# A decoder layer on one core: the factors of four norms spread by float32r high and low diagonals of 512 columns, and the recurrence's statistics later

## The chip, the cores and the metric

The kernel runs on one core of a Trainium2 chip. The metric is device time in microseconds of one execution. A core has TensorE (PE: matmuls into PSUM, with weight loads, PEld, that overlap them), VectorE (DVE), ScalarE (ACT), GpSimd (POOL) and SyncE (SP, which here issues DMAs). Each engine works through its own queue in order and waits on semaphores for the others.

## What is computed

One layer for a sequence of 512 tokens with 1024 features: a half-step SwiGLU FFN of 2816 hidden features, a mixer, and a second half-step FFN. Each of the three is wrapped in two RMS norms, one on its input and one on its output before it is added to the stream. Inside the mixer the recurrence's output and the attention's output, 512 features each, have a norm of their own:

```python
def rms_norm(x, g):
    y = x * lax.rsqrt(jnp.mean(x * x, axis=-1, keepdims=True) + 1e-6)
    return y * g

def hybrid_mixer(h, ...):
    x_lru, gate_lru, q, k, v = split(h @ w_in)
    y_lru = rg_lru(x_lru, ...) * gelu(gate_lru)          # 512 features
    y_attn = sliding_window_sink_attention(q, k, v, sinks)
    y = concatenate([rms_norm(y_lru, g_lru_out), rms_norm(y_attn, g_attn_out)])
    return y @ w_o

x = x + 0.5 * rms_norm(swiglu(rms_norm(x, ffn1_pre_g), ...), ffn1_post_g)
x = x + rms_norm(hybrid_mixer(rms_norm(x, mix_pre_g), ...), mix_post_g)
x = x + 0.5 * rms_norm(swiglu(rms_norm(x, ffn2_pre_g), ...), ffn2_post_g)
```

All inputs and the output are fp32.

## The kernel before

**Layout and precision.** Activations are kept turned: features on the 128 partitions, 512 tokens along the free axis (`T`; `NB` = 4 blocks of 128 tokens, `KD` = 8 chunks of 128 features, `KC` = 4). To keep fp32 precision at float32r's matmul rate, each operand is split into a high part (rounded to float32r) and a low part (the rest), and a product is three matmuls: high by high, high by low, low by high (`mm3`).

**Norms.** A norm's factor belongs to a token, that is, to a column in this layout, so a number for each token has to reach all 128 partitions. `InvRms` does that for half the tokens (256) at a time:
- `stats` takes a bank of PSUM and turns the sums of squares (`acc`, features on partitions) into means with tokens on partitions: one matmul of one column (fp32, with `acc` as the weights) for each block of 128 tokens.
- `invert` takes the square root (ACT) and the reciprocal (DVE), and makes the diagonal: the identity times the factor, 128 x 256 in fp32 (DVE).
- `spread` multiplies the diagonal with a matrix of ones in one fp32 matmul of 256 columns, which leaves every token's factor on all partitions. In the profile an fp32 matmul appears as two records.

`Next` is the norm ahead of a sub-layer. Its inputs go through the products unscaled; the factors are copied to a tile `R` (ACT, `Next.spread`) and multiplied in afterwards (DVE). There are three: `n1` (name `a`, bank `rms_x`, whose statistics `InvRmsX.early` takes from sums over the rows of x), `mx` (the mixer's input) and `n2` (`f2`). The recurrence's norm, `lru`, uses `InvRms` as well, without a copy: DVE multiplies `hl` by the PSUM bank. The norms on the sub-layers' outputs (`Residual`) use `InvRms` too.

**Order.** All engines' orders are written out by hand: an engine executes its instructions in the order in which the program issues them. `Weights` (`W`) streams weights from HBM into a ring of raw tiles (SP's queue); a unit's `cast` (ACT) makes the high part and `tensor_sub` (mostly DVE) the low part. `W.fill(n)` prepares units until n are ready beyond those taken, `W.round` casts one, `W.take` hands one out; the next raw load is issued when the last unit of a raw tile has its low part.

**Around the recurrence's norm.** The output product `y @ w_o` runs over eight output chunks c. For the first five (`EARLY`) the attention's half is multiplied first (`wo_attn`: high parts by both weight parts for each k, then low parts). For c = 0 to 2 together these are 36 matmuls, then come the statistics of `lru` (both halves) and `W.fill(3)`; then c = 3 (12 matmuls), the two spreads and, on DVE and ACT, the scaled outputs `ylh` and `yll` of the recurrence; then c = 4 (12 matmuls), and then the recurrence's half for all five (`mm3` over k = 0, 1, and then 2, 3). The rest of `w_o` and the next sub-layer's start are in `boundary`.

Of the kernel before, what the change touches and what calls it, by code (L numbers as in the profile page):

```python
# [23 lines left out]
KC = C // P  # L24
# [98 lines left out]
def tile_layer(ctx: ExitStack, tc: tile.TileContext, out: bass.AP, **ins: bass.AP):  # L123
    nc = tc.nc
    pe, dve, act, pool, sync = nc.tensor, nc.vector, nc.scalar, nc.gpsimd, nc.sync

    const = ctx.enter_context(tc.tile_pool(name="const", bufs=1))
# [3 lines left out]
    small = ctx.enter_context(tc.tile_pool(name="small", bufs=4))  # L131
# [5 lines left out]
    ALL = slice(0, T)  # L137
# [348 lines left out]
    def preload(func):  # L486
        act.activation(dummy, eps, func)
# [9 lines left out]
    def col(name, i):  # L497
        return colrange(name)[:, i:i + 1]
# [40 lines left out]
    def square(src, sl, name, scale=1.0):  # L539
        sq = wt(f"sq_{name}")[:, sl]  # L540
        act.activation(sq, src, AF.Square, scale=scale)  # L541
        return sq

    class InvRms:


        def __init__(self, accs, mean, half, name, eps=eps):
            self.accs, self.mean, self.half, self.name, self.eps = accs, mean, half, name, eps

        def stats(self):  # L550
            self.ps = ps = bank(f"rms_{self.name}")
            for i in range(2):
                b = 2 * self.half + i
                for j, a in enumerate(self.accs):
                    pe.matmul(ps[:, i:i + 1], a[:, b * P:(b + 1) * P], self.mean, start=j == 0, stop=j == len(self.accs) - 1)
            self.invert(ps[:, :2])

        def invert(self, ms, scale=1.0):
            n = self.name
            rms = small.tile([P, 2], F32, tag="rms", name=f"rms_s{n}")  # L560
            act.activation(rms, ms, AF.Sqrt, bias=self.eps, scale=scale)
            rs = small.tile([P, 2], F32, tag="rs", name=f"rs_{n}")
            dve.reciprocal(rs, rms)
            self.dg = wt(f"dg_{n}", T)[:, :2 * P].rearrange("p (a b) -> p a b", a=2)
            dve.tensor_tensor(self.dg, ident.unsqueeze(1).to_broadcast([P, 2, P]), rs.unsqueeze(2).to_broadcast([P, 2, P]), op=ALU.mult)

        def spread(self):
            o = self.ps[:, T // 2:]
            pe.matmul(o, ones, self.dg.rearrange("p a b -> p (a b)"), start=True, stop=True)
            return o  # L570


    def stream():
# [10 lines left out]
    def x_high(x, src, gain, sl):  # L584
        act.activation(x[0][:, sl], src, AF.Copy, scale=gain)

    def x_low(x, src, gain, sl):
        dve.scalar_tensor_tensor(x[1][:, sl], src, gain, x[0].bitcast(F32)[:, sl], op0=ALU.mult, op1=ALU.subtract)
# [13 lines left out]
    class Next:  # L602


        def __init__(self, name, pre=None, gain=None):
            self.name, self.pre = name, pre
            self.gain = gain or (lambda c: col(pre, c))
            self.t = {}
            self.xs = x_parts(name)
            self.acc = tmp.tile([P, T], F32, tag="acc", name=f"acc_n{name}", bufs=3)  # L610
            self.rms = [InvRms([self.acc], mean_d, h, f"n{name}{h}") for h in range(2)]
            self.R = None

        def high(self, c, h):
# [10 lines left out]
                    dve.tensor_add(self.acc, self.acc, square(xT[c], ALL, f"n{self.name}{c}"))  # L625

        def stats(self):
            for h in range(2):
                self.rms[h].stats()

        def spread(self):
            if self.R is None:
                self.R = big.tile([P, T], F32, tag="R", name=f"R_{self.name}")
                for h in range(2):
                    act.copy(self.R[:, HALF[h]], self.rms[h].spread())

        def sums(self, k):

# [555 lines left out]
        hi, lo, raw = piece(j, i)  # L1194
        eng.tensor_sub(lo, raw, hi.bitcast(F32))

    class InvRmsX(InvRms):


        def early(self):  # L1200
            b = 4 * self.half
            ss = small.tile([P, 2], F32, tag="ss", name=f"ss_{self.name}")
            sx = ssx[:, b:b + 4].rearrange("p (b h) -> p b h", h=2)
# [6 lines left out]
    n1.rms = [InvRmsX(None, None, h, f"x{h}") for h in range(2)]  # L1210


    warm = bank("warm")
# [54 lines left out]
    for r in n1.rms:  # L1268
        r.early()
# [50 lines left out]


    gw, home = {}, []
    v4 = lambda t: t.rearrange("p (a b) -> p a b", a=NB)
    up8 = t2k("up8", U8).rearrange("p (a b) -> p a b", a=NB)
    up8f = up8.rearrange("p a b -> p (a b)")

# [311 lines left out]
    hl = us_  # L1638
# [218 lines left out]
    def add_square(ci):  # L1857
        if ci == 0:
            act.activation(accl, hl[0], AF.Square)
        else:  # L1860
            dve.tensor_add(accl, accl, square(hl[ci], ALL, f"l{ci}"))

    for ci in range(KC):
        add_square(ci)
    preload(AF.Sqrt)
    lrms = [InvRms([accl], mean_c, h, f"lru{h}") for h in range(2)]

    res = Residual("r2", lambda c: col("mix_post_g", c))
    EARLY = KD - LATE

    def wo_attn(cs):
        ks = range(KC, KD)
        for k in ks:
            for c in cs:
                for part in ws[c]:
                    pe.matmul(banks[c], part[:, k, :], ysp[k][0], start=k == KC and part is ws[c][0], stop=False)
        for c in cs:
            for k in ks:
                pe.matmul(banks[c], ws[c][0][:, k, :], ysp[k][1], start=False, stop=False)

    ws, banks = [], []
    for c in range(EARLY):
        ws.append(W.take(0))
        banks.append(bank(f"wo{c}"))
        if c < EARLY - 3:
            continue
        wo_attn(range(c + 1) if c == EARLY - 3 else [c])
        if c == EARLY - 3:
            for l in lrms:
                l.stats()  # L1890
            W.fill(3)
        if c == EARLY - 2:
            bcs = [l.spread() for l in lrms]
            for ci in range(KC):
                for h in range(2):
                    dve.tensor_mul(hl[ci][:, HALF[h]], hl[ci][:, HALF[h]], bcs[h])
                y = t2k(f"ylh{ci}", F32R), t2k(f"yll{ci}", F32R)
                x_high(y, hl[ci], col("g_lru_out", ci), ALL)
                x_low(y, hl[ci], col("g_lru_out", ci), ALL)
                ysp[ci] = y  # L1900
    for k in (0, 1):
        for c in range(EARLY):
            mm3(banks[c], ws[c], k, ysp[k], False, False)
# [202 lines left out]
```

## Time and profile before

| | us |
|---|---|
| median of 3 runs | 839.75 |
| lowest, highest | 839.74, 840.31 |
| the profiled execution | 839.52 |
| its span, first to last instruction | 837.6 |
| TensorE busy | 829.3 |
| VectorE busy | 730.5 |
| ScalarE busy | 520.0 |
| GpSimd busy | 166.4 |

The profiled execution's mean granted TensorE clock is 0.998 of full speed. In the rows of the timeline the first column is the start in us from the span's start, the second the time in us, then engine, line, operation, out<-in, sizes and how many instructions the row merges; square brackets hold the idle time of the engine just before it and what ended it. Records of matmuls overlap, because they are pipelined. Busy times are averages over stages with different limits; what counts at a place is which engine comes last there.

### The profile page before, as it was taken

The page shows a single profiled execution, that of the slowest core. Times are in us where ns is not written, and L with a number is a line of the kernel's source. Part 1 is how long each engine was busy: PE and PEld are TensorE (multiplying, and loading weights), DVE is VectorE, ACT ScalarE, POOL GpSimd, SP SyncE. Part 2 cuts the span into 40 slices and gives each one's busy share as a digit, 9 for nine tenths or more (in the row PEclk, how much of TensorE's full clock was granted, in tenths as well). Part 3 has the DMA queues.
Part 4 walks back from the last instruction along what each step waited for, and adds up shares of the span by engine and source line. Part 5 has one row for each costly group of instructions (what it writes and reads, how often), then busy time and mean ns, then how long its engine had stood idle before and what let it go on. Part 6 is the DMA issues. An engine that isn't in the chain of part 4 may idle for free.

```text
span 837.6 us, 11902 instructions
## 1 busy us (share of the span) xinstructions
PE 829.3 (99%) x4252; PEld 705.7 (84%) x4252; DVE 730.5 (87%) x1036; ACT 520.0 (62%) x813; POOL 166.4 (20%) x188
## 2 busy tenths in 40 slices
PE   9999999999999999999999999999999999999996
PEld 8988888888888898987788899888888888888885
DVE  4989799998989978888789589997999799898996
ACT  6656656676666654556797446545757667676562
POOL 2022000140320325414531042002005023032001
PEclk9999999999999999999999999999999999999999
DMA  7376408398595797522511130657339939769742
GB/s 253 102 266 236 147 10 302 97 264 261 124 259 183 186 280 235 181 93 78 163 47 51 51 124 30 129 173 251 110 114 244 312 85 256 238 155 259 299 142 101
DMA packets 121851, 144.22 MB, mean 172 GB/s; under 512 B 24184, under 2 KB 76736, under 8 KB 121280
## 3 DMA queue, kind: packets, MB, share of 16 engines
q1 hardware_dynamic: 107824, 112.91, 42.0%
q0 software_dynamic: 13824, 30.42, 16.5%
q8 instruction: 33, 0.54, 0.3%
q14 instruction: 26, 0.21, 0.1%
q10 hardware_dynamic: 144, 0.13, 0.0%
HBM read 100.45 MB, written 39.32 MB: 167 GB/s over the span
## 4 chain that ended last, share of the span: by engine, by line
PE 96%; DVE 2%; DMA 1%; SPq 0%; issue 0%; ACT 0%; DVEq 0%; ACTq 0%
PE ab L968 10%; PE aa L968 10%; PE db L968 5%; PE da L968 5%; PE yaa L1362 3%; PE bb L968 3%; PE ba L968 3%; PE ya L1362 3%; PE yda L1362 2%; PE aa L898 1%; PE a_first L1230 1%; PE yab L1945 1%; PE yab L1946 1%; PE yab L1947 1%; PE yea L1362 1%; PE yba L1362 1%
## 5 line engine op out<-in xcount | busy, mean ns | idle before, releaser
L1140 POOL DMA_DIRECT2D yr_a<-stage x36 | 31.6, 1013 | 176.8 <-ACT stage L1137 155.9
L1140 POOL DMA_DIRECT2D yp_b<-stage x42 | 36.5, 1046 | 147.0 <-ACT stage L1137 118.2
L1961 POOL DMA_DIRECT2D yp_b<-stage x8 | 4.3, 546 | 65.3 <-ACT stage L1960 64.8
L691 POOL TENSOR_TENSOR acca_r<-acca_r,sq_r 128x512 f32<-128x512 f32 x6 | 9.0, 1498 | 40.0 <-ACT sq_r L541 39.9
L529 PE MATMUL an<-xh_mx,whi_xl 128*128 128x256 f32 x64 | 15.9, 288 | 0.0
L530 PE MATMUL an<-xh_mx,wlo_xl 128*128 128x256 f32 x64 | 15.5, 283 | 0.0
L2061 ACT ACTIVATE ysq<-yp 128x512 f32<-128x512 f32 (+1 forms) x8 | 4.9, 606 | 16.7 <-DVE yp L2054 16.7
L2064 POOL TENSOR_TENSOR last<-yp,grow 128x512 f32<-128x512 f32 x3 | 3.9, 1293 | 56.2 <-DVE yp L2054 56.2
L511 PE MATMUL gt<-xh_mx,whi_gt 128*128 128x512 f32 x32 | 14.3, 447 | 0.0
L1399 POOL DMA_DIRECT2D yp_a<-zy x16 | 8.8, 555 | 25.4 <-DMA rows_a<-yr_a 17.2
L511 PE MATMUL pq<-xh_mx,whi_q 128*128 128x512 f32 x32 | 12.8, 400 | 0.0
L511 PE MATMUL pub<-xh_f,whi_bu 128*128 128x512 f32 x32 | 12.6, 395 | 0.0
L513 PE MATMUL gt<-xh_mx,wlo_gt 128*128 128x512 f32 x32 | 12.6, 394 | 0.0
L511 PE MATMUL pgb<-xh_f,whi_bg 128*128 128x512 f32 x32 | 12.6, 393 | 0.0
L512 PE MATMUL gt<-xl_mx,whi_gt 128*128 128x512 f32 x32 | 12.5, 392 | 0.0
L512 PE MATMUL pq<-xl_mx,whi_q 128*128 128x512 f32 x32 | 12.5, 391 | 0.0
L513 PE MATMUL pq<-xh_mx,wlo_q 128*128 128x512 f32 x32 | 12.5, 390 | 0.0
L513 PE MATMUL pgb<-xh_f,wlo_bg 128*128 128x512 f32 x32 | 12.5, 390 | 0.0
L513 PE MATMUL pub<-xh_f,wlo_bu 128*128 128x512 f32 x32 | 12.5, 390 | 0.0
L512 PE MATMUL pub<-xl_f,whi_bu 128*128 128x512 f32 x32 | 12.5, 390 | 0.0
L512 PE MATMUL pgb<-xl_f,whi_bg 128*128 128x512 f32 x32 | 12.5, 389 | 0.0
L1362 PE MATMUL ya<-whi_ad,hha 128*128 128x512 f32 x32 | 12.4, 389 | 0.0
(2018 smaller groups left out, 3412.7 us busy)
## 6 DMA issues: line engine op xcount, KB each, us to landing
yp_b<-stage POOLq DMA_DIRECT2D x50, 256.0 KB, 9.2
yr_a<-stage POOLq DMA_DIRECT2D x44, 256.0 KB, 9.8
h_a<-za SPq DMA_DIRECT2D x16, 256.0 KB
h_b<-zb SPq DMA_DIRECT2D x16, 256.0 KB
hxb<-h_b SPq DMA_DIRECT2D x16, 256.0 KB
hxa<-h_a SPq DMA_DIRECT2D x6, 512.0 KB
xn<-in_x SPq DMA_DIRECT2D x8, 256.0 KB
raw_ad<-in_ffn_w_down SPq DMA_DIRECT2D x2, 1024.0 KB
```

Of the source, the lines that this page charges most:

```text
L511: pe.matmul(ps, hi[:, k, :], xh, start=start, stop=False)
L512: pe.matmul(ps, hi[:, k, :], xl, start=False, stop=False)
L513: pe.matmul(ps, lo[:, k, :], xh, start=False, stop=stop)
L529: pe.matmul(ps[:, sl], hi[:, k, :], xh, start=k == 0 and not goes_on, stop=False, skip_group_check=True)
L530: pe.matmul(ps[:, sl], lo[:, k, :], xh, start=False, stop=False, skip_group_check=True)
L691: eng.tensor_add(acc, acc, square(part, ALL, f"{self.name}{c}"))
L898: pe.matmul(o, w[:, k, js], x, start=first and i + j + k == 0, stop=k == 3 and i == 2, skip_group_check=True)
L968: pe.matmul(b[tb], x[:, blk], w[:, k, :], start=first and q + k + j == 0, stop=q + k == 2 and j == 2, skip_group_check=True)
L1140: pool.dma_start(o, st, accum_op=ALU.add)
L1230: pe.matmul(banks[j][:, HALF[0]], ws[j][part][:, k, :], n1.xs[k][xpart][:, HALF[0]], start=k == 0 and part == xpart, stop=stop and k == KD ...
L1362: pe.matmul(o, x[:, blk], a[:, k, :], start=start and j == 0, stop=stop and j == 2, skip_group_check=True)
L1399: (pool if q % 2 else sync).dma_start(chunks[32 * q:32 * (q + 1), :, i * P:(i + 1) * P], turned[32 * i:32 * (i + 1), :, q])
```

## The change

For the three `Next` norms and for `lru` a new class, `InvRmsRows`, takes all 512 tokens at once. One bank instead of two, four statistics matmuls into it, one square root of four columns, one reciprocal. The factor is then split into a float32r high part (the diagonal made from the factor itself is rounded as it is written) and a low part (factor less rounded factor), and two diagonals of 128 x 512 in float32r are made. Spread is two float32r matmuls of 512 columns into the same bank, added up. `ones` becomes a float32r tile; the output norms keep `InvRms` with the same values read as fp32. `R` is filled by one ACT copy of 512 columns instead of two of 256, and `hl` is multiplied in one DVE operation of 512 columns instead of two.

```diff
-    ones = filled("ones", P, 1.0)
+    ones = const.tile([P, P], F32R, name="ones")
+    dve.memset(ones.bitcast(F32), 1.0)
...
+    class InvRmsRows:
+        def __init__(self, acc, mean, name):
+            self.acc, self.mean, self.name = acc, mean, name
+        def stats(self):
+            self.ps = ps = bank(f"rms_{self.name}")
+            for b in range(NB):
+                pe.matmul(ps[:, b:b + 1], self.acc[:, b * P:(b + 1) * P], self.mean, start=True, stop=True)
+            self.invert(ps[:, :NB])
+        def invert(self, ms, scale=1.0):
+            n = self.name
+            rms, rs, low = (small.tile([P, NB], F32, tag=t, name=f"{t}_{n}", bufs=1) for t in ("rms4", "rs4", "rl4"))
+            high = small.tile([P, NB], F32R, tag="rh4", name=f"rh4_{n}", bufs=1)
+            act.activation(rms, ms, AF.Sqrt, bias=eps, scale=scale)
+            dve.reciprocal(rs, rms)
+            dve.tensor_copy(high, rs)
+            dve.tensor_sub(low, rs, high.bitcast(F32))
+            self.dg = [wt(f"d{i}_{n}", T, F32R) for i in "hl"]
+            for d, r in zip(self.dg, (rs, low)):
+                dve.tensor_tensor(v4(d), ident.unsqueeze(1).to_broadcast([P, NB, P]), r.unsqueeze(2).to_broadcast([P, NB, P]), op=ALU.mult)
+        def spread(self):
+            for i, d in enumerate(self.dg):
+                pe.matmul(self.ps, ones, d, start=i == 0, stop=i == 1)
+            return self.ps
...
     class Next:
-            self.rms = [InvRms([self.acc], mean_d, h, f"n{name}{h}") for h in range(2)]
+            self.rms = InvRmsRows(self.acc, mean_d, f"n{name}")
...
-                for h in range(2):
-                    act.copy(self.R[:, HALF[h]], self.rms[h].spread())
+                act.copy(self.R, self.rms.spread())
```

`InvRmsX` derives from the new class and adds its row sums for all four blocks in one operation. Around the recurrence's norm the order changes as well: one `w_o` unit is cast (`W.round`) ahead of the square root's table load; the statistics come two matmuls into c = 3, the spread with the recurrence's outputs two matmuls into c = 4; of the two units that `W.fill(3)` prepared, one is finished behind c = 2 and the other behind the outputs.

```diff
     for ci in range(KC):
         add_square(ci)
+    W.round()
     preload(AF.Sqrt)
-    lrms = [InvRms([accl], mean_c, h, f"lru{h}") for h in range(2)]
+    lrms = InvRmsRows(accl, mean_c, "lru")
...
-    def wo_attn(cs):
+    def wo_attn(cs, between=lambda: None):
         for k in ks:
             for c in cs:
                 for part in ws[c]:
                     pe.matmul(banks[c], part[:, k, :], ysp[k][0], ...)
+            if k == KC:
+                between()
...
-        wo_attn(range(c + 1) if c == EARLY - 3 else [c])
         if c == EARLY - 3:
-            for l in lrms:
-                l.stats()
-            W.fill(3)
-        if c == EARLY - 2:
-            bcs = [l.spread() for l in lrms]
-            (the outputs, product in halves)
+            wo_attn(range(c + 1))
+            W.fill(2)
+        elif c == EARLY - 2:
+            wo_attn([c], lrms.stats)
+        else:
+            wo_attn([c], spread_lru)
+    W.fill(1)
```

`spread_lru` spreads and makes the outputs as before, with the product over all 512 columns.

More of the change, by code (lines that the diff above doesn't have):

```diff
@@ L568, in spread @@
             o = self.ps[:, T // 2:]
-            pe.matmul(o, ones, self.dg.rearrange("p a b -> p (a b)"), start=True, stop=True)
+            pe.matmul(o, ones.bitcast(F32), self.dg.rearrange("p a b -> p (a b)"), start=True, stop=True)
             return o
+    class InvRmsRows:
[21 more added lines that the diff above has]
+            return self.ps
     def stream():
@@ L1208, in stats @@
             self.ps = bank(f"rms_{self.name}")
[L1210 removed]
+    n1.rms = InvRmsX(None, None, "x")
     warm = bank("warm")
@@ L1879, in wo_attn, with spread_lru @@
                 pe.matmul(banks[c], ws[c][0][:, k, :], ysp[k][1], start=False, stop=False)
+    def spread_lru():
+        bc = lrms.spread()
+        for ci in range(KC):
+            dve.tensor_mul(hl[ci], hl[ci], bc)
+            y = t2k(f"ylh{ci}", F32R), t2k(f"yll{ci}", F32R)
+            x_high(y, hl[ci], col("g_lru_out", ci), ALL)
+            x_low(y, hl[ci], col("g_lru_out", ci), ALL)
+            ysp[ci] = y
     ws, banks = [], []
```

22 lines of the change are left out of this document (6 added, 16 removed).

## The prediction

> **What bounds the kernel now.** I read the page first (engines, chain), then the waits of TensorE, then the timeline of each engine around the four norms.
>
> ```profile
> span 837.6 us, 11902 instructions
> ...
> PE 829.3 (99%) x4252; PEld 705.7 (84%) x4252; DVE 730.5 (87%) x1036; ACT 520.0 (62%) x813; POOL 166.4 (20%) x188
> ...
> DMA packets 121851, 144.22 MB, mean 172 GB/s; under 512 B 24184, under 2 KB 76736, under 8 KB 121280
> ...
> PE 96%; DVE 2%; DMA 1%; SPq 0%; issue 0%; ACT 0%; DVEq 0%; ACTq 0%
> ```
>
> The chain that ended last is 96% TensorE, and TensorE is busy 99% of the span. So a shorter TensorE slot shortens the run, as long as no other engine becomes late in its place; what is done on VectorE (DVE), ScalarE (ACT) or GpSimd (POOL) counts only where TensorE then waits. In the view of TensorE's waits only one lies inside the run, at the norm that the change moves:
>
> ```profile
> PE rms_lru L555 <- DVE acc_lru L1861: 0.3, 1, 0.3
> ```
>
> The steady pace of a 128x512 float32r matmul, and the slots of the four fp32 spreads (each row: four records, two for each half), from the timeline of TensorE:
>
> ```profile
> 469.02 0.39 PE L511 MATMUL wo<-ylh,whi_wo 128*128 128x512 f32 x1
> ...
> 476.95 0.39 PE L513 MATMUL wo<-ylh,wlo_wo 128*128 128x512 f32 x1
> ...
> 28.61 1.02 PE L569 MATMUL rms_x<-dg_x,ones 128*128 128x256 f32 x4
> 29.59 0.28 PE L530 MATMUL a_first<-xh_a,wlo_first 128*128 128x256 f32 x1
> ...
> 373.05 1.02 PE L569 MATMUL rms_nmx<-dg_nmx,ones 128*128 128x256 f32 x4
> 374.15 0.40 PE L512 MATMUL pv<-xl_mx,whi_kv 128*128 128x512 f32 x1
> ...
> 465.39 1.02 PE L569 MATMUL rms_lru<-dg_lru,ones 128*128 128x256 f32 x4
> 466.49 0.40 PE L1876 MATMUL wo<-attn,wlo_wo 128*128 128x512 f32 x1
> ...
> 530.85 1.03 PE L569 MATMUL rms_nf<-dg_nf,ones 128*128 128x256 f32 x4
> 531.95 0.40 PE L512 MATMUL pub<-xl_f,whi_bu 128*128 128x512 f32 x1
> ```
>
> From 469.02 to 476.95 us are 35 steps of back-to-back matmuls: 0.2266 us each, though each record is 0.39 us long, since they overlap. So slots have to be read from start to start. The last row of each pair is the second matmul after the spread; between lie the spread and one ordinary matmul.
>
> **The change part by part.**
>
> *Spread.* Removed are two fp32 matmuls of 256 columns for each norm. Their slot is 374.15 - 373.05 - 0.23 = 0.87 us; the recurrence's (466.49 - 465.39) and the last norm's (531.95 - 530.85) come to the same. In the first norm the neighbours have 256 columns and a step of 0.12 (half of 0.23): 29.59 - 28.61 - 0.12 = 0.86. Added are two float32r matmuls of 512 columns, 2 x 0.2266 = 0.45. Saving: 3 x 0.42 + 0.41 = 1.67 us on TensorE. The weights are `ones` before and after.
>
> For this price the Trainium skill has a rule ("TensorE: Matmul & The Clock Gate", section Back-to-back issue gap): a sustained stream with N=512 runs at about 131 ns for each matmul. By it the two added matmuls would cost 0.26, and the sum would gain another 0.76; the trace shows 0.2266 for exactly this shape, and that is used.
>
> *Statistics.* Four one-column fp32 matmuls stay. Only in the recurrence's norm (`lru`) do they move: behind two more matmuls of c=3.
>
> ```profile
> 369.37 0.95 PE L555 MATMUL rms_nmx<-mean_d,acc_nmx 128*128 128x1 f32 x8
> ...
> 370.50 0.40 PE L512 MATMUL pk<-xl_mx,whi_kv 128*128 128x512 f32 x1
> ...
> 460.46 0.84 PE L1879 MATMUL wo<-yal,whi_wo 128*128 128x512 f32 x3
> 461.60 1.05 PE L555 MATMUL rms_lru<-mean_c,acc_lru 128*128 128x1 f32 x8 [0.30 <-DVE acc_lru L1861]
> ...
> 462.84 0.40 PE L1876 MATMUL wo<-attn,wlo_wo 128*128 128x512 f32 x1
> ```
>
> ```profile
> 459.27 2.27 DVE L1861 TENSOR_TENSOR acc_lru<-acc_lru,sq_l 128x512 f32<-128x512 f32 x3
> ...
> 462.54 0.17 DVE L563 RECIPROCAL rs_lru<-rms_slru 128x2 f32<-128x2 f32 x1 [0.99 <-ACT rms_slru L561]
> 462.81 0.42 DVE L565 TENSOR_TENSOR dg_lru<-ident,rs_lru 128x256 f32<-128x256 f32 x1
> ...
> 463.92 2.36 DVE L215 TENSOR_TENSOR wlo_wo<-raw_wo__4185,whi_wo 128x1024 fp32r<-128x1024 f32 x2
> 466.20 0.74 DVE L1896 TENSOR_TENSOR xc<-xc,rms_lru 128x256 f32<-128x256 f32 x2
> ...
> 467.74 0.75 DVE L588 SCALAR_TENSOR_TENSOR yll<-xc,cols,ylh 128x512 fp32r<-128x512 f32 x1 [0.79 <-ACT ylh L585]
> ```
>
> The three matmuls from 460.46 on would let the next begin at 461.14. The statistics began at 461.60, and from there to the second matmul behind them it took 1.24 where the undisturbed norm took 370.50 - 369.37 = 1.13. So the wait costs 0.46 + 0.11 = 0.57 us. VectorE ends the sum of squares at 461.54. With two matmuls more in front the statistics come at 461.14 + 0.45 = 461.59: the wait is all but gone, perhaps not the 0.11 of a weight load that could not be fetched ahead. I take a gain of 0.45 (bounds 0.3 and 0.57).
>
> *The longer way to the diagonals.* Square root, reciprocal, copy, subtract and two products of 512 columns now follow one another. Sizes:
>
> ```profile
> 462.24 0.26 ACT L561 ACTIVATE rms_slru<-rms_lru,eps 128x2 f32<-128x2 f32 x1 [0.65 <-PE rms_lru L555]
> 462.69 0.26 ACT L561 ACTIVATE rms_slru<-rms_lru,eps 128x2 f32<-128x2 f32 x1 [0.18 <-PE rms_lru L555]
> ...
> 466.98 0.72 ACT L585 ACTIVATE ylh<-xc,cols 128x512 fp32r<-128x512 f32 x1 [2.14 <-DVE xc L1896]
> ```
>
> ```profile
> 374.52 1.30 DVE L1495 TENSOR_TENSOR xp<-an,R_mx 128x512 f32<-128x512 f32 x2 [1.36 <-ACT R_mx L635]
> ...
> 570.04 0.69 DVE L824 TENSOR_TENSOR u<-pub,R_f 128x512 f32<-128x512 f32 x1 [1.48 <-PE pub L513]
> ```
>
> ```profile
> L1636 DVE TENSOR_TENSOR xc<-xc,th x4: 679/681/1155, 438.0 to 445.3; 128x512 f32<-128x512 f32 x4
> ```
>
> Let S be the start of the statistics. All eight records of them end at S+1.05; the root follows at S+1.09 (462.69 against 461.60) and lasts 0.26; the reciprocal follows 0.04 later, at S+1.39. From the reciprocal to its product is 0.27, so with 0.27 each for reciprocal, copy and subtract the high diagonal begins at S+2.20, the low one 0.61 later (1.30 for two, 0.69 for one) at S+2.81, and ends at S+3.50. The copy and the subtract have no row of their own; the bounds are 0.17 (the reciprocal's length) and 0.42 (a 256-column product), which put the end at S+3.3 and S+3.8. A disturbed product of 512 columns is the exception (of four in the last row the median is 0.68 and the longest 1.16); with two such the end is S+4.5. TensorE comes to the first spread after twelve matmuls in all three norms that have statistics on TensorE: S + (1.13 - 0.23) + 12 x 0.2266 = S+3.62, and to the second, which reads the low diagonal, at S+3.85. Cover 0.35, so the cost is nothing; it is up to 0.6 at a place where both products are disturbed. In the first norm the factors come from row sums, and the diagonals stand in VectorE's order well ahead of the spread: nothing.
>
> *Behind the spread.* In the mixer's input norm (`mx`) one ACT copy of 512 columns replaces two of 256; with ACT's 0.72 it ends at 373.05 + 0.23 + 0.39 + 0.04 + 0.72 = 374.43, before the 374.52 at which VectorE took `R`. VectorE's diagonals ended at about S+2.1 before (462.69 + 0.26 + 0.04 + 0.27 + 0.42, less 461.60), so its work behind them comes 1.4 us later; it had 1.36 us of idle time there and starts up to 0.1 later, while TensorE is 0.42 earlier: a lag of 0.4 to 0.5. Its tightest reader is the gate product of the recurrence:
>
> ```profile
> 396.23 2.07 POOL L1534 TENSOR_TENSOR xcl<-xc,xch 128x512 fp32r<-128x512 f32 x1 [1.08 <-ACT xch L1533]
> ...
> 398.82 0.39 PE L1515 MATMUL rg<-xcl,gates 64*128 64x512 f32 x1
> ```
>
> There 398.82 - 398.30 = 0.52 us are left, so nothing is lost, by a hair. In the last norm (`f2`) VectorE is also 1.4 us late behind the diagonals; the 1.48 at 570.04 is an idle time in which it waits for TensorE again. TensorE has no wait in between, so I put nothing; uncovered, it could cost up to 1.4.
>
> *The recurrence's outputs.* Before, twelve matmuls lay between spread and the first reader of `ylh0`; now ten: from the first spread at s, 0.45 + 10 x 0.2266 = s+2.72 for the high part, s+2.95 for the low. The second spread ends at s + 0.23 + 0.39 = s+0.62; then the 512-column product 0.69, the high part 0.72, the low part 0.75, with 0.04 before each: high at s+2.11, low at s+2.90. It fits by 0.05, so I take 0, with 0 to 0.4 as bounds (0.4 with a product of 1.16). The product of 512 columns (0.69) replaces 0.74 of two halves.
>
> *Moved weight work.* One rounding of a `w_o` tile goes before the table load of the square root. ACT had 0.65 idle before the first root, and its one root now comes at 461.59 + 1.09 = 462.68, 0.44 later: 1.09 of room.
>
> ```profile
> 466.31 0.37 SPq L175 DMA_DIRECT2D raw_bu__4859<-in_ffn_w_gu  x1
> ...
> 488.75 1.04 ACT L210 CAST whi_bu<-raw_bu__4859 128x1024 fp32r<-128x1024 f32 x1
> ```
>
> A cast takes 1.04: it fits, by 0.05. Its low part (2.36 / 2 = 1.18) falls into VectorE's 0.99 + 0.44 of idle time. The other tile's cast and low part go behind the four outputs, to about 476, and with them the load that their raw buffer frees, from 466.31 on SP's queue to about 476. Its data are cast at 488.75; at the page's mean of 172 GB/s 1 MB (128 x 2048 fp32) takes about 6 us (an estimate), so the 12 us left hide it.
>
> **Sum.** 1.67 + 0.45 = 2.12 us. The profiled execution took 839.52 us (span 837.6 and 1.9 outside, which the change doesn't touch): 837.40. The runs' median, 839.75, is 0.23 above it, so 837.6. About 0.2% (1.68 us) can be told from no change.
>
> **Rivals.**
>
> *Given back in part.* The margins above are thin: 0.05 at `yll0`, 0.05 at the root, 0.52 against up to 0.5 at `xcl`. If they fail, the prices are up to 0.4 at the outputs, 0.42 at `mx`, 0.45 if the statistics still wait. For it: VectorE at 87% and the wait that exists is on VectorE. Against: TensorE shows no other wait. All three: a gain of 0.85, 838.9; one of them, 838.1.
>
> *Slower: the low diagonal comes later than its spread.* Place: second spread of `mx`, `lru` and `f2`, behind which all of TensorE queues. Nothing is lost up to S+3.85; beyond it each 0.1 costs 0.3. The gain is gone at S+4.56, and slower by 1.68 needs S+5.12, which would be 839.75 + 1.7 = 841.4. Against: even two disturbed products end at S+4.5.
>
> *The spread is no cheaper.* The Trainium skill ("Perfetto Trace Analysis", section Engine Utilization) divides the systolic array's output rate by 2 for FP32_LOW_HIGH. By that two fp32 spreads of 256 columns equal two float32r ones of 512, and the spread would give nothing. As a mechanism of this kernel: only the wait's 0.45 is left, 839.3. Against: the slot of 0.87 is almost twice 0.45.
>
> **How the numbers follow.** Forecast 0.66; in part 0.27; spread no cheaper 0.02; slower 0.05. Faster by over 0.2% is the forecast's case: 0.66; same 0.27 + 0.02 = 0.29; slower 0.05. Range: down to 837.0, which takes in the whole 0.57 of the wait and the 0.57 by which the runs before differ (839.74 to 840.31); up to 838.9, all of the partial rival.
>
> **What would show it.** Right: two records of 512 columns at each of the four spreads, with the neighbours 0.45 apart for them; no TensorE wait at `rms_lru`; no new wait on `ylh`, `yll`, `xcl` or a diagonal. Wrong: a TensorE wait at one of these, a statistics wait that stays, or the second spread starting over 0.3 us behind the first.

## The result, and the profile after

The kernel after took 837.45 us (median of 8 runs, 837.34 to 837.96), the kernel before 839.8 (8 runs, 839.34 to 840.31). The ratio is 0.9973, with an interval of 0.9964 to 0.9981: faster by 0.27%. The profiled execution took 837.42 us; 837.40 was forecast for it, and 837.6 for the median.

The page of the kernel after (span, engines, shares of the chain that ended last):

```profile
span 835.6 us, 11875 instructions
...
PE 827.5 (99%) x4244; PEld 704.3 (84%) x4244; DVE 732.7 (88%) x1035; ACT 518.8 (62%) x806; POOL 165.9 (20%) x188
...
PE 98%; DMA 1%; DVE 0%; SPq 0%; issue 0%; DVEq 0%
```

and the view of TensorE's waits, whole (line, what was waited for, us in total, times, longest):

```profile
PE warm L1247 <- POOL ident masks.py:199: 1.4, 1, 1.4
PE xtp L1195 <- DMA xn<-in_x: 0.4, 1, 0.4
```

The wait at `rms_lru` is gone from this view (0.12 us of it is left, as shown below), and the two that it lists lie in the first 10 us. Two of the four spreads, in TensorE's timeline (start, us, then engine, line, operation):

```profile
372.21 0.39 PE L602 MATMUL rms_nmx<-dh_nmx,ones 128*128 128x512 f32 x1
372.44 0.39 PE L602 MATMUL rms_nmx<-dl_nmx,ones 128*128 128x512 f32 x1
372.67 0.40 PE L512 MATMUL pv<-xh_mx,whi_kv 128*128 128x512 f32 x1
...
464.61 0.39 PE L602 MATMUL rms_lru<-dh_lru,ones 128*128 128x512 f32 x1
464.83 0.40 PE L602 MATMUL rms_lru<-dl_lru,ones 128*128 128x512 f32 x1
465.06 0.39 PE L1905 MATMUL wo<-yah,whi_wo 128*128 128x512 f32 x1
```

Each spread is an ordinary step of 0.23 us, twice, with no wait between them; those of x and f2 take the same. The profile's busy times say little about such a change; a ledger says more. At each place below, the start of the same TensorE instruction was read in two profiles, and the table gives by how many us the kernel after is ahead of the kernel before. The kernel after was profiled a second time in the last experiment.

| place | before at | after ahead by | after, second profile |
|---|---|---|---|
| 16 transposes ahead of the first norm | 20.96 | 0.25 | 0.26 |
| spread of x | 28.61 | 0.40 | 0.41 |
| statistics of mx | 369.37 | 0.84 | 0.87 |
| second matmul behind mx's spread | 374.15 | 1.25 | 1.27 |
| last transposes of the probabilities (`pt`) | 442.04 | 1.24 | 1.28 |
| the next matmul (`gt`) | 442.46 | 0.80 | 1.27 |
| first matmul of `w_o` | 452.98 | 0.82 | 1.25 |
| first reader of `ylh0` | 469.02 | 1.66 | 2.11 |
| statistics of f2 | 527.17 | 1.57 | 2.01 |
| second matmul behind f2's spread | 531.95 | 1.97 | 2.41 |
| last matmul | 830.99 | 1.96 | 2.41 |

The four norms are where the forecast put the gain. Two steps are not in it: 0.40 us are there before the first spread, and 0.44 are lost between two neighbouring instructions in the attention, in the first profile but not in the second. The experiments were made to tell whether these belong to the change.

### The profile page after: what moved, and what is told of

Read it like the earlier page. It is cut to its first block, busy times and chain, and to the rows that moved or that the text cites. A ratio compares the mean times of both kernels' runs of the same rounds, so it can differ in the third digit from the quotient of the medians.

```text
span 835.6 us, 11875 instructions
## 1 busy us (share of the span) xinstructions
PE 827.5 (99%) x4244; PEld 704.3 (84%) x4244; DVE 732.7 (88%) x1035; ACT 518.8 (62%) x806; POOL 165.9 (20%) x188
## 4 chain that ended last, share of the span: by engine, by line
PE 98%; DMA 1%; DVE 0%; SPq 0%; issue 0%; DVEq 0%
PE aa L999 10%; PE ab L999 10%; PE db L999 5%; PE da L999 5%; PE yaa L1390 3%; PE ba L999 3%; PE bb L999 3%; PE ya L1390 3%; PE yda L1390 2%; PE aa L929 1%; PE a_first L1260 1%; PE yab L1981 1%; PE yab L1979 1%; PE yab L1980 1%; PE wo L1905 1%; PE gt L512 1%
```

## Experiments

Runs made together share a chip and the runs of the kernel before; others may not, so small differences are read inside profiles. There, "length" is the time from the 16 transposes ahead of the first norm to the last matmul, which leaves the start-up out: 810.03 before, 808.32 and 807.88 in the two profiles after.

**The order alone.**

```diff
 (kernel before; condensed)
+    W.round()
     preload(AF.Sqrt)
...
-        wo_attn(range(c + 1) if c == EARLY - 3 else [c])
+        if c == EARLY - 3: wo_attn(range(c + 1)); W.fill(2)
+        elif c == EARLY - 2: wo_attn([c], stats_lru)     # fp32 halves as before
+        else: wo_attn([c], spread_lru)
+    W.fill(1)
```

> The kernel before, with only the recurrence's norm in its new order (rounding ahead of the table load, statistics two matmuls later, spread two matmuls into the next output block); all four spreads stay two fp32 matmuls of 256 columns. Theory 'the terms add': the statistics' wait of 0.57 us goes, 0.45 to 0.57 us faster than before (839.3 against 839.8); from the last matmul before the statistics to the first one behind the two spreads TensorE's slots lose 0.45 to 0.57, the spread's slot stays 0.87. Rival 'the order only pays with the cheaper spread' (the dearer spread and eight half products make the outputs late): no gain, and a stall of 0.3 us or more at the first reader of yll0.

838.96 us, where the kernel before, run beside it, took 839.23 (ratio 0.9996, 0.9987 to 1.0005). In its profile TensorE is 0.66 behind the profile before at the first matmul of `w_o` and 0.25 behind at the first reader of `ylh0`: the new order alone gains 0.41, with no wait at the outputs. The term stands, a little under the 0.45 to 0.57 expected; the times by themselves don't tell this kernel from the one before. The 0.66 behind come from elsewhere: 0.23 stood already at `mx`, from the start-up, and 0.44 come from the same transposes in the attention as in the kernel after, where this kernel is the kernel before, instruction by instruction:

```profile
442.28 1.10 PE L1714 MATMUL pt<-ident,sc 128*128 128x128 f32 x4
```

So that loss is no effect of the change.

**The spreads alone.**

```diff
 (kernel after; condensed)
-    W.round()
     preload(AF.Sqrt)
...
-        if c == EARLY - 3: wo_attn(range(c + 1)); W.fill(2)
-        elif c == EARLY - 2: wo_attn([c], lrms.stats)
-        else: wo_attn([c], spread_lru)
-    W.fill(1)
+        wo_attn(range(c + 1) if c == EARLY - 3 else [c])
+        if c == EARLY - 3: lrms.stats(); W.fill(3)
+        if c == EARLY - 2: spread_lru()
```

> The kernel after, with the recurrence's norm put back in its old order (statistics behind two matmuls fewer, both roundings behind it, spread behind the whole fourth output block). Theory 'the terms add': the four spreads give 3 x 0.42 + 0.41 = 1.67 us as matmul slots and the statistics wait again for about 0.5 us, so 0.45 to 0.57 slower than after. If the attention's stall of 0.5 us at the last transposes of the probabilities stays as in the profile after, that makes 837.9 to 838.0; without it 837.5. Rival 'the spreads are cheap only in the new order': 1 us or more slower than after.

838.36 us (ratio to before 0.999, 0.9981 to 0.9999). At the norm itself both theories miss. TensorE's lead goes from 0.59 at the first matmul of `w_o` to 1.03 at the first reader of `ylh0` (the spread, 0.44), and then falls to 0.48: 0.87 less than the kernel after gains there, not 0.45 to 0.57. VectorE's and TensorE's timelines of this kernel:

```profile
463.48 0.68 DVE L598 TENSOR_TENSOR dl_lru<-ident,rl_lru 128x512 fp32r<-128x512 f32 x1
464.08 2.35 DVE L215 TENSOR_TENSOR wlo_wo<-raw_wo__4179,whi_wo 128x1024 fp32r<-128x1024 f32 x2
466.35 0.68 DVE L1914 TENSOR_TENSOR xc<-xc,rms_lru 128x512 f32<-128x512 f32 x1
```

```profile
460.99 1.05 PE L585 MATMUL rms_lru<-mean_c,acc_lru 128*128 128x1 f32 x8 [0.28 <-DVE acc_lru L1889]
...
464.99 0.40 PE L602 MATMUL rms_lru<-dl_lru,ones 128*128 128x512 f32 x1
...
468.63 0.50 PE L513 MATMUL wo<-yll,whi_wo 128*128 128x512 f32 x1 [0.26 <-DVE yll L621]
```

The spread is done at 465.39, but VectorE is still with the low parts of two weight tiles, which stand behind the longer way to the diagonals, and takes the factors up at 466.35. So the two halves of the change lean on each other: the new order, which takes these low parts out of the way, is worth 0.41 with the fp32 spreads and 0.87 with the new ones. The attention's transposes lose nothing here (0.41 to the next matmul).

**The recurrence's products later.** The stall in the attention was first put down to VectorE: the last unit's row maxima stand behind two products that overlap a GpSimd select.

```diff
             scores(*units[now])
             if now == 7:
                 for ci in (2, 3):
+                    root_u(ci)
+                for ci in (2, 3):
                     scan(ci)
...
-        if now == 6:
-            for ci in (2, 3):
-                root_u(ci)
```

> The kernel after, with the products of the recurrence's root and input for blocks 2 and 3 moved on VectorE from ahead of the last attention unit's scores to behind them. Theory 'the transposes of the last unit stalled 0.5 us because that unit's row maxima come late on VectorE and meet a GpSimd select': the maxima's scaled minimum is written 1.3 us or more earlier, the four transposes take 0.36 us from their first to the next matmul instead of 0.85, and the run is 0.4 to 0.5 us faster than after (837.0). Rival 'given back later' (the sum of squares of the recurrence is the bound 20 us on): TensorE gains at the transposes, then waits at the recurrence's statistics for the same 0.4 to 0.5 us, and the time stays 837.4.

837.47 us (ratio 0.9978, 0.9969 to 0.9987), no better than after. The transposes now take 0.35 us to the next matmul, but 0.28 is given back, 7 us on and not at the statistics. VectorE, with the products behind the scores, comes to the next unit's output at 443.26 instead of 442.66 (0.34 of that is the later start-up of this profile). TensorE, which loses nothing at the transposes of the probabilities, comes to those of the attention's rows at 447.89 instead of 448.10, but VectorE's scaling of the second block ends no earlier than before, at 448.55 (448.48 in the kernel after). The fifth of the eight transposes waits for it.

```profile
448.07 0.48 DVE L1794 TENSOR_SCALAR home<-home,rat 128x512 f32<-128x512 f32 x1
```

```profile
447.89 1.37 PE L1852 MATMUL atp<-ident,home 128*128 128x128 f32 x8
449.10 1.24 PE L1852 MATMUL atp<-ident,yn 128*128 128x128 f32 x8
```

From the first to the second row are 1.21 us; in the kernel after they were 0.93. Whether moving the products ended the stall isn't shown by this run: `nm`, the instruction on which the stall hangs (see below), took 0.16 us in its profile and wasn't held either.

**The mixer's input norm as before.**

```diff
+            self.halves = [InvRms([self.acc], mean_d, h, f"n{name}{h}") for h in range(2)] if name == "mx" else None
...
-                act.copy(self.R, self.rms.spread())
+                (for mx) act.copy(self.R[:, HALF[h]], self.halves[h].spread())   # h = 0, 1
```

> The kernel after, with the mixer's input norm alone put back to two fp32 spreads of 256 columns. Theory 'its saving of 0.42 is kept': 0.42 slower than after (837.9), with the same stall of 0.5 us at the last unit's transposes. Rival 'its saving is what the attention gives back' (TensorE gained 0.42 there and lost 0.45 at the transposes): the stall is at most 0.1 us, and the time is that of after within 0.1 us.

837.99 us (ratio 0.9985, 0.9977 to 0.9994). TensorE's lead stays at 0.96 across this norm, and the stall at the transposes is there again (0.86 to the next matmul). The length is 808.65, 0.33 more than after. So `mx`'s saving is kept, and it isn't what the attention gives back: the rival falls.

**What the stall hangs on.** With these profiles the stalls could be sorted by one pair of instructions 12 us ahead of it: VectorE's scaled minimum `nm` of unit (2, 1) and GpSimd's select `pp` of unit (2, 0). First the two profiles of the kernel after, the stalled one ahead:

```profile
428.33 0.64 DVE L1721 SCALAR_TENSOR_TENSOR nm<-mx,nsink 128x4 f32<-128x4 f32 x1
```

```profile
428.32 0.63 POOL L1748 TENSOR_SCALAR_AFFINE_SELECT pp<-pa 128x512 f32<-128x512 f32 x1 [1.87 <-DVE mx L1715]
```

```profile
440.81 1.10 PE L1742 MATMUL pt<-ident,sc 128*128 128x128 f32 x4
```

```profile
428.29 0.16 DVE L1721 SCALAR_TENSOR_TENSOR nm<-mx,nsink 128x4 f32<-128x4 f32 x1
```

```profile
440.76 0.67 PE L1742 MATMUL pt<-ident,sc 128*128 128x128 f32 x4
```

In the first, GpSimd started 10 ns ahead, and `nm`, 4 columns wide, took 0.64 us instead of 0.16: it ended when the select did. ScalarE's exponentials, its table loads and roots, and through them GpSimd's later selects then run 0.5 us late. So a later select runs into the first of the recurrence's two products (L1664), and the next one into the last unit's `nm`. VectorE's timeline, the stalled profile ahead:

```profile
436.74 1.61 DVE L1664 TENSOR_TENSOR xc<-xc,th 128x512 f32<-128x512 f32 x2
...
439.98 0.32 DVE L1721 SCALAR_TENSOR_TENSOR nm<-mx,nsink 128x4 f32<-128x4 f32 x1
```

```profile
436.74 1.29 DVE L1664 TENSOR_TENSOR xc<-xc,th 128x512 f32<-128x512 f32 x2
...
439.65 0.16 DVE L1721 SCALAR_TENSOR_TENSOR nm<-mx,nsink 128x4 f32<-128x4 f32 x1
```

Of the 0.48 by which the last `nm` ends late, the product brings 0.32 and `nm` itself 0.16. Which of the two instructions comes first is a draw of a few ns. Two kernels are to force it:

```diff
+        if (b, n) == (2, 0):
+            act.copy(dummy, eps)
         act.copy(pa, pt)
```

> The kernel after, with one copy of a single column put on ScalarE ahead of the copy of the probabilities of unit (block 2, half 0), so that GpSimd's select of that unit starts some 0.1 us later. Theory 'a draw of 10 ns between VectorE's scaled minimum nm and GpSimd's select decides whether TensorE stalls 0.45 us some 12 us later' (VectorE first in the profiles before, order only and spread only: stall at most 0.06; GpSimd first in the profiles after, order only and mx as before: 0.44 or 0.45): here VectorE is always first, nm takes 0.16 us, and the last four transposes of the probabilities take at most 0.45 us to the next matmul; 0 to 0.45 us faster than after, by how often after loses the draw. Rival 'the stall comes from the products of root and input that overlap the select': the stall stays at 0.85 us whatever nm takes.

```diff
-                dve.tensor_reduce(mx_[:, 2 * i:2 * i + 2], cur, op=ALU.max, axis=AX.X)
+                for _ in range(2 if (b, n, i) == (2, 1, 1) else 1):
+                    dve.tensor_reduce(mx_[:, 2 * i:2 * i + 2], cur, op=ALU.max, axis=AX.X)
```

> The kernel after, with the last row maximum of unit (block 2, half 1) taken twice on VectorE, so that its scaled minimum nm comes 0.35 us later and GpSimd's select is always first. Theory of the draw: nm is held until the select ends, the exponentials that wait for it come 0.8 us after the copy of the probabilities, and the last four transposes take 0.8 us or more to the next matmul in this profile; up to 0.45 us slower than after, and 0.4 to 0.5 slower than the kernel with the select later. Rival (the products): nothing of this moves with nm, and both kernels show the same stall.

Select later: 837.29 us (6 runs; ratio 0.9968, 0.9956 to 0.9981). Minimum later: 837.77 (11 runs; 0.9978, 0.9970 to 0.9987), on the same chip: 0.48 apart, though the intervals of the two ratios overlap, and the lengths are 807.94 and 808.41. The rows, of the first and of the second kernel:

```profile
428.75 0.16 DVE L1721 SCALAR_TENSOR_TENSOR nm<-mx,nsink 128x4 f32<-128x4 f32 x1
```

```profile
441.17 0.68 PE L1742 MATMUL pt<-ident,sc 128*128 128x128 f32 x4
```

```profile
441.33 1.10 PE L1743 MATMUL pt<-ident,sc 128*128 128x128 f32 x4
```

In the second kernel ScalarE's exponentials wait 0.81 us for `nm` (0.24 in the first). `nm` itself shows 0.18 us there: the second maximum alone puts it back by 0.46. So this kernel shows what a late `nm` costs, and not that the select held it; that is shown by the 0.64 of the other profiles. The theory of the products falls as the cause, since in both kernels the products stand where they stood. They are a link of the chain: the first of them takes 0.68 us in the kernel with the select later and 1.04 in the one with the minimum later.

Over all 13 profiles the sorting has no exception if it goes by what `nm` took. Held for 0.64 us (after, order only, mx as before, low diagonal delayed twice) or put back (minimum later): 0.85 or 0.86 us from the transposes to the next matmul. `nm` at 0.16 (the other eight): 0.35 to 0.44. (What was expected of the kernel with the select later names "order only" on both sides; it is one of the stalled.) By the starts there is one exception: in the profile before, the select's record starts 5 ns ahead of `nm`'s, yet `nm` took 0.16 and the select 0.67. So a few ns between two records don't tell which came first, and the times taken do.

**The low diagonal later.**

```diff
-            for d, r in zip(self.dg, (rs, low)):
+            more = 0 if n == "x" else 1          # and 2
+            for d, r in zip(self.dg[:1] + self.dg[1:] * (1 + more), (rs,) + (low,) * (1 + more)):
```

> The kernel after, with the low diagonal of the three norms that have statistics on TensorE (mx, lru, f2) written twice, so that it ends one product of 512 columns (0.61 us) later. Measured ends in the profile after: 3.06, 3.13 and 3.07 us after the start of the statistics; here 3.67, 3.74 and 3.68. Theory 'threshold at 3.85': the second spread still begins 0.23 us behind the first in mx and f2, no loss there; in lru too, but its outputs come no later, since they wait for the spread. Rival 'the low diagonal already sets the second spread': each second spread begins 0.4 to 0.6 us later, 1.2 to 1.8 us in all.

> The kernel after, with the low diagonal of mx, lru and f2 written three times, so that it ends two products (1.22 us) later: 4.28, 4.35 and 4.29 us after the start of the statistics, 0.4 to 0.5 us beyond the threshold of 3.85. Theory: TensorE waits at each second spread, which then begins 0.7 to 0.8 us behind the first instead of 0.23; 1.3 to 1.6 us lost in the three. Rival 'work behind the diagonals on VectorE is the tighter bound': the loss shows at other places (the first reader of xcl, of yll0, of the first products of f2) and already in the kernel with one delay.

One run each: 837.39 and 840.11 us. A second write of the same tile took 0.73 us, not 0.61. With one, the low diagonal ends at 3.79 (mx) and 3.87 (lru) after the statistics' start, and from the second spread to the next matmul are 0.26 and 0.31 us: the threshold lies about where it was put, at 3.85. But the length is 808.22, 0.34 more than in the second profile after, for which no loss was expected: 0.04 to 0.07 stand behind each spread, and 0.17 at the four transposes of v (`vt`), which start 0.50 behind the matmul ahead of them instead of 0.31 because VectorE's `vT` comes too late. So in `mx` the rival is right: the work behind the diagonals is the tighter bound, at a reader that it didn't name. With two the low diagonal ends at 4.52 (mx), and TensorE's waits name it (`rms_nmx` of this kernel):

```profile
372.22 0.40 PE L603 MATMUL rms_nmx<-dh_nmx,ones 128*128 128x512 f32 x1
373.11 0.51 PE L603 MATMUL rms_nmx<-dl_nmx,ones 128*128 128x512 f32 x1 [0.49 <-DVE dl_nmx L599]
373.45 0.39 PE L512 MATMUL pv<-xh_mx,whi_kv 128*128 128x512 f32 x1
```

The pair takes 1.23 us instead of 0.46: 0.66 later for the second spread, and 0.11 more behind it (0.34 to the next start instead of 0.23), as at the statistics before. The length is 810.80, 2.5 more than in the first profile after, which lost at the transposes too (1.3 to 1.6 were expected, with 0.61 for each write). So the rival of a slower kernel was real as a mechanism, with the forecast threshold, and 0.1 dearer for each norm than its price; the kernel after stays 0.7 us clear of it at the spreads.

**One fp32 matmul of 512 columns.**

```diff
-            self.dg = [wt(f"d{i}_{n}", T, F32R) for i in "hl"]
-            for d, r in zip(self.dg, (rs, low)):
+            self.dg = [wt(f"d_{n}", T)]
+            for d, r in zip(self.dg, (rs,)):
...
-                pe.matmul(self.ps, ones, d, start=i == 0, stop=i == 1)
+                pe.matmul(self.ps, ones.bitcast(F32), d, start=True, stop=True)
```

> The kernel after, with each spread as one fp32 matmul of 512 columns on one fp32 diagonal (no split, no low diagonal). Theory 'an fp32 matmul takes four passes of its columns': the spread's slot is 4 x 0.2266 = 0.91 us, or 0.87 as two of 256 took, 0.42 to 0.46 dearer than the two float32r ones; 1.7 us slower than after in the four norms. Rival 'two instructions cost twice one, whatever the type': the slot is 0.45 us or less, and the time that of after.

One run: 838.13 us; the length is 809.34, 1.46 more than in the second profile after (1.7 was expected).

```profile
529.46 1.02 PE L599 MATMUL rms_nf<-d_nf,ones 128*128 128x512 f32 x2
...
530.55 0.39 PE L513 MATMUL pub<-xl_f,whi_bu 128*128 128x512 f32 x1
```

The slot is 530.55 - 529.46 - 0.23 = 0.86 us, the same as two fp32 matmuls of 256 took. It is the type and the columns that cost, not the number of instructions: a column costs 3.8 times as much in fp32 as in float32r. The Trainium skill ("FP8 and Floating Point Precision", section TensorE Precision Notes) gives true fp32 four passes through the array; 3.8 is a little under that. Its division by 2, which was a rival ("Perfetto Trace Analysis", section Engine Utilization), does not hold between these two types.

**After again, and a version with both waits moved.** The second kernel is the one with the select later, and

```diff
-            wo_attn([c], lrms.stats)         # behind 2 matmuls of c = 3
+            wo_attn([c], lrms.stats, 3)      # behind 3
-            wo_attn([c], spread_lru)         # behind 2 matmuls of c = 4
+            wo_attn([c], spread_lru, 1)      # behind 1
```

> The kernel after once more, on the same chip as the kernel with the select later and the new places of statistics and spread, to compare with it and for another draw. Theory: its 16 transposes ahead of the norm of the input take 1.66 us to the next matmul (1.80 and 1.78 in the two profiles with two roots there), the draw decides over 0.45 us at the last unit's transposes, and the rest of its profile agrees with the first within 0.1 us from stage to stage.

> The kernel with the select later, and in the recurrence's norm the statistics one matmul later and the spread one matmul earlier. In the profile after the statistics still begin 0.12 us behind their slot and the second matmul that reads yll0's block begins 0.08 late; the low diagonal ends 3.13 us after the statistics' start, and the second spread would now come 3.39 after it. Theory: both small waits go, 0.2 us less between the last transposes of the attention and the last matmul of the block than in the kernel with the select later; against after 0.2 us, and 0.65 where after loses the draw. Rival 'VectorE has no room left': the wait appears at the second spread, and nothing is gained.

After again: 837.35 us (10 runs, 836.29 to 838.32; ratio 0.9974, 0.9964 to 0.9983). Its profile is the last column of the ledger: the same from stage to stage within 0.06 us, but for the transposes. The new version: 836.81 us (6 runs, 836.33 to 837.31; ratio 0.9969, 0.9957 to 0.9981). Its length is 807.71, 0.17 less than the second profile after, 0.61 less than the first, and 0.23 less than the kernel with the select later (0.2 was expected). The second spread follows the first by 0.22, so VectorE has room left. Both small waits are gone: the statistics begin 0.23 behind the matmul ahead of them, and the readers of the outputs go in step:

```profile
466.84 0.39 PE L513 MATMUL wo<-yll,whi_wo 128*128 128x512 f32 x1
467.07 0.39 PE L514 MATMUL wo<-ylh,wlo_wo 128*128 128x512 f32 x1
```

In the profiles it beats the kernel after; in the times its median is 0.54 lower, but the intervals of the two ratios overlap.

## Why the prediction was right, step by step

**Spread.** 1.67 forecast; 0.40, 0.41, 0.41 and 0.40, together 1.62, measured. The Trainium skill's figure of 131 ns for each matmul ("TensorE: Matmul & The Clock Gate", section Back-to-back issue gap), which the prediction set beside its sum, doesn't hold for this stream: the steps are 0.23.

**Statistics.** 0.45 forecast; 0.41 in the kernel with the order alone, and 0.84 - 0.42 = 0.42 in the kernel after, whose statistics still begin 0.12 behind their slot:

```profile
460.55 0.39 PE L1905 MATMUL wo<-attn,wlo_wo 128*128 128x512 f32 x1
460.90 1.02 PE L585 MATMUL rms_lru<-mean_c,acc_lru 128*128 128x1 f32 x8
```

The prediction left a rest of this kind open ("perhaps not the 0.11 of a weight load that could not be fetched ahead").

**The longer way to the diagonals.** No cost, as forecast, but the size was off, and outside its bounds: the end was put at S+3.50, between S+3.3 and S+3.8, and came at S+3.06, 3.13 and 3.07. TensorE came to the second spread at S+3.91 to 3.93, where S+3.85 was forecast. VectorE's timeline at `lru`, where S = 460.90:

```profile
462.25 0.18 DVE L593 RECIPROCAL rs_lru<-rms_lru 128x4 f32<-128x4 f32 x1 [0.36 <-ACT rms_lru L592]
462.47 0.17 DVE L594 CAST rh_lru<-rs_lru 128x4 fp32r<-128x4 f32 x1
462.67 0.16 DVE L595 TENSOR_TENSOR rl_lru<-rs_lru,rh_lru 128x4 f32<-128x4 f32 x1
462.75 0.69 DVE L598 TENSOR_TENSOR dh_lru<-ident,rs_lru 128x512 fp32r<-128x512 f32 x1
463.35 0.68 DVE L598 TENSOR_TENSOR dl_lru<-ident,rl_lru 128x512 fp32r<-128x512 f32 x1
```

The step that was mis-sized is "0.27 each for reciprocal, copy and subtract": they took 0.22, 0.20 and 0.08. The high diagonal doesn't read what the subtract makes, so it follows at the distance of two instructions that don't depend on each other; the prediction priced it as a dependent one.

**Behind the spread.** Nothing was lost, as forecast, but not for the reasons given. In `mx` VectorE still waits 0.41 for `R` (1.36 before), so the longer diagonals delay nothing there. The lag is ScalarE's: `R` is ready 1.25 after the start of the spread (1.43 before), while TensorE's second matmul behind the spread starts 0.69 after it (1.10 before). That is a lag of 0.2 rather than 0.4 to 0.5. And the tightest reader isn't that of `xcl`, where 0.31 of the 0.52 is left, but the transposes of v, which the prediction doesn't have. VectorE and TensorE, before:

```profile
384.86 0.68 DVE L1487 TENSOR_TENSOR vT<-pv,R_mx 128x512 f32<-128x512 f32 x1
```

```profile
385.82 0.66 PE L1575 MATMUL vt<-ident,vT 128*128 128x128 f32 x4
```

and after:

```profile
383.82 0.68 DVE L1515 TENSOR_TENSOR vT<-pv,R_mx 128x512 f32<-128x512 f32 x1
```

```profile
384.57 0.66 PE L1603 MATMUL vt<-ident,vT 128*128 128x128 f32 x4
```

`vT` ended 0.28 ahead of its reader and now ends 0.07 ahead. Where the low diagonal was written twice, `vt` waited and started 0.06 behind the end of `vT`. So the cover was all but used up, and a lag of 0.4 to 0.5, as forecast, would have cost about 0.2 here (an estimate: the lag, less the 0.22 between 0.28 and 0.06). Two errors met, and that this term came out at nothing is in part luck. In `f2` VectorE's idle time ahead of the product `u` at 570.04 was 1.48 and is 0.41: the diagonals did push it, and the cover held.

**Outputs.** Forecast: "fits by 0.05", cost 0. Readiness was right almost to the digit (s+2.89 against s+2.90), the reader's place was s+2.98 instead of s+2.95, and the margin was too thin after all:

```profile
466.75 0.75 DVE L621 SCALAR_TENSOR_TENSOR yll<-xc,cols,ylh 128x512 fp32r<-128x512 f32 x1 [0.79 <-ACT ylh L618]
```

```profile
467.58 0.47 PE L513 MATMUL wo<-yll,whi_wo 128*128 128x512 f32 x1
467.89 0.40 PE L514 MATMUL wo<-ylh,wlo_wo 128*128 128x512 f32 x1
```

`yll0` ends at 467.50, its reader starts at 467.58, and the next matmul 0.31 later instead of 0.23; why a reader that starts behind the end of its input still loses this stays open. This 0.08 is all that came of the rival "given back in part". With the spread one matmul earlier it is gone.

**Moved weight work.** The cast and the table load end 0.2 us ahead of the root, and SP issues the freed buffer's load at 475.37 (about 476 forecast); no wait followed.

**What the prediction didn't have.** Three things. First, a gain of 0.13 at the norm of x, which it put at nothing outside the spread. Before, ScalarE had two roots there, and the second waited for VectorE while the turned chunks stood behind it (ScalarE, before):

```profile
22.05 0.30 ACT L561 ACTIVATE rms_sx<-ss_x,eps 128x2 f32<-128x2 f32 x1 [0.83 <-DVE ss_x L1204]
22.25 3.01 ACT L585 ACTIVATE xh_a<-xtp,g 128x256 fp32r<-128x256 f32 x8
```

After, there is one root, and the high parts wait for TensorE alone:

```profile
20.66 0.30 ACT L592 ACTIVATE rms_x<-ss_x,eps 128x4 f32<-128x4 f32 x1
21.35 3.03 ACT L618 ACTIVATE xh_a<-xtp,g 128x256 fp32r<-128x256 f32 x8 [0.40 <-PE xtp L1195]
```

From the 16 transposes to the next matmul TensorE takes 1.80 and 1.78 us in the two profiles with two roots, and 1.66 or 1.67 in the eleven with one. Second, the start-up: the 16 transposes begin between 20.25 and 21.37 us over the 13 profiles, whatever the kernel, and the first profile after was 0.25 luckier than the one before. Third, the draw in the attention, which it lost and the profile before had won: 0.44. Together: 2.12 - 0.05 (spread) - 0.03 (statistics) - 0.08 (outputs) + 0.13 + 0.25 - 0.44 = 1.90, where the last matmul came 1.96 earlier. The second profile after, which won the draw, is 2.15 shorter in length than the profile before, where the terms without start-up and draw give 2.09. The forecast's own terms came to 1.96 (1.62 + 0.42 - 0.08), so their sum, 2.12, was good to 0.2, and that the profiled execution came out within 0.02 us of its forecast is chance: neither start-up nor draw is in the forecast. The kernel with the order alone, unchanged up to that place, lost the draw as well; whether the change shifts the odds of it isn't shown.

## What to carry to other kernels

When an engine is full, price an edit there in steps from start to start, and give each helper engine a margin from the place where its result is due; here margins of 0.35 us and more held, of two of 0.05 one did not, and one of 0.28 that the prediction hadn't priced was left with 0.07. So look for the tightest reader of all that an engine makes behind the change, not only of the one in view. A change that lengthens a chain on another engine may need that engine's queue cleared around it: the spread without the new order lost 0.55 us at its outputs. A difference below 0.1% between two profiles should be looked for in a second profile of the same kernel before it is explained: the largest unforeseen step here was in five of 13 profiles, among them one of a kernel that has that stretch unchanged.

## What the runs showed of the hardware

- A VectorE instruction of 4 columns with two inputs takes 0.16 us, and 0.64 when a GpSimd select of 512 columns has started 6 to 10 ns ahead of it (four profiles); it ends as the select ends. The Trainium skill has this rule ("SBUF — State Buffer", section Who interferes with whom): a VectorE instruction with two inputs in SBUF and a GpSimd instruction that reads SBUF exclude each other, and the one that issues first keeps the port for its whole length. The traces agree, as far as starts a few ns apart can be told (the profile before, with 5 ns, is the exception above), and they add what it can cost: 0.5 us on ScalarE, and 0.44 on TensorE 12 us later.
- A TensorE wait can cost about 0.1 us beyond its own length, at the step behind it: 0.11 at a spread that waited. An output that ended 0.08 ahead of its reader's start still cost 0.08 there.
- On VectorE, starts of small dependent instructions are 0.20 to 0.22 us apart, of independent ones 0.08; two writes of 512 columns to the same tile are 0.73 apart, to different tiles 0.60.
